# Causal convolution taps of two channel groups moved to GpSimd, their norm issued after the chunks of the sample attention, and one power operation for four row tiles

## The chip, the cores and the metric

The kernel runs on one core of a Trainium2 chip (trn2). The metric is the time of one execution in microseconds (us). A core has five engines with a queue each, which they work through in order: PE (TensorE: matmuls and transposes; PEld is its weight load), DVE (VectorE), ACT (ScalarE), POOL (GpSimd) and SP (SyncE, which here issues nearly all DMAs).

## The reference, cut to what matters

One layer of a hybrid decoder for 512 prompt rows and 64 sample rows (8 sequences of 8 new tokens). After a norm, one input projection feeds two groups. Group A is latent attention; the sample rows attend over 2048 cached keys in pages of 128. Group B is a gated linear unit, a causal depthwise convolution of width 31 over 512 channels, a norm over the channels and a swish. Both groups go through one output projection, and a gated feed-forward network follows.

```python
D_CQ = 384; D_C = 256; D_CONV = 512; CONV_W = 31
def mixer_inputs(h, pos, w_in, g_q_norm, w_uq, g_kv_norm, w_uk):
    proj = h @ w_in
    cq, ckv, kr, glu_in = ...
    q = jnp.einsum('btc,chd->bthd', rmsnorm(cq, g_q_norm), w_uq)
    kv_rows = jnp.concatenate([rmsnorm(ckv, g_kv_norm), kr], axis=-1)
    glu = glu_in[..., :D_CONV] * jax.nn.sigmoid(glu_in[..., D_CONV:])
def conv_module(glu, prev, w_dw, b_dw, g_ln, b_ln):
    y, new_prev = causal_dwconv(glu, prev, w_dw, b_dw)
    return jax.nn.silu(layernorm(y, g_ln, b_ln)), new_prev
# merge: x + concat(rmsnorm(attn), rmsnorm(conv_y)) @ w_o, then the gated network
```

`rmsnorm` and `layernorm` need the power -0.5 of a mean per row.

## The kernel before, in words

Rows come in five tiles (`TILES`: four of 128 prompt rows, one of 64 sample rows); channels of the convolution in four groups `m` of 128, one on each partition. Matmuls run on numbers split into a high and a low part, so most tiles are copied (`split`: ACT copies the high part, L110; DVE subtracts, L111).

The order of work is: input norm; the latent columns of the projection (`latent_cols`) and the GLU columns (`glu`, one group `m` at a time); the latent norms and transposes per row tile (`latent`); queries; then the sample attention; then the prompt attention by heads; the output projection; the feed-forward network, which takes the second half of the time.

The **convolution** of group `m` over the prompt is 31 taps, each a multiply-add of 512 elements on each partition (`conv_taps`, L239 to L250). On DVE a tap is one instruction (L246). On POOL it is two: the product into a temporary `ct` (L249) and the sum (L250); the first tap of a chain is one instruction (L244). The constants `NV0`, `NV2`, `NV3`, `NG2` divide the taps: group 0 has 20 on DVE and 11 on POOL into a second accumulator `acc2`; group 1 has all 31 on POOL; group 2 has 12 on DVE before the sample attention, 15 more on DVE inside it, one per chunk (the list `later`), and the last four on POOL into `acc2`; group 3 has all 31 on POOL. The chains on POOL are issued after the last power operation so far (`tc.issue_after(last["pow"])`). POOL adds `acc2` at L988 when chunk 21 comes. The sample rows' part of the convolution is `conv_sample` on DVE (L258 to L262).

The **power operation** is `rstd_of` (L116 to L120): DVE scales, POOL raises to -0.5 (L119). `latent(i)` calls it for each row tile.

The **sample attention** has 32 chunks of 512 keys (loop over `J`, `slot(J)`). A chunk transposes its keys on PE into `ktb`, splits them (`kh` on ACT, `kl` on DVE), multiplies with the queries into `sb` (L585 to L588), takes the running maximum on DVE (L592), and for the sequence before it the exponential (ACT, L607), transposes of the probabilities (`ptb`), the split of the values (`ch` on ACT, L637; `cl` on DVE, L638) and the product with the values (`ob`, L647 to L655). The pages are loaded by SP, seven chunks ahead.

The **norm of the convolution** is `conv_norm` (L746 to L781): for each row tile transposes to rows (`lnb`), statistics on DVE, a power operation on POOL, the scaling on ACT (L763), transposes back (`lnt`) and a copy on ACT (L747); then the swish (L769); then per row tile transposes (`lns`), a sum of squares (L776) and another power operation. Its steps are issued two per chunk from chunk `CN0` = 21 on. `conv_scaled` (L835, L836) makes the left operand of `proj_conv`, which projects the conv rows between the heads of the prompt attention; `wob` is its bank. The prompt attention starts with `open_right` at chunk 33, whose eight POOL memsets (L793, L794) clear parts of the value tiles `vh` and `vl` that the products `pv` read.

The tile `gx` holds the GLU output of all four groups. Its memory is given to the weights `wv` at chunk 30 (tag `gx`), which therefore wait until the taps have read it, and later to a part of the attention's output (`atp`).

The order within each engine's queue is not written out: a planner that models the engines fixes it before the run. It takes what its model says is ready, by a priority that follows the program's order, shifted by the entries of `PR` under which a step is issued (`cn` is -150, `later` +80).

Of the kernel before, what the change touches and what calls it, by code (L numbers as in the profile page):

```python
# [15 lines left out]
ALU = mybir.AluOpType  # L16
# [47 lines left out]
def hymba_step(ctx, tc, x, cache, pt, sconv, sffn, vec, rows, w1, wglu, wuq, wuk, wuv, wukT,  # L64
# [8 lines left out]
    # ------------------------------------------------------------------ helpers  # L73
# [71 lines left out]
    # ------------------------------------------------------------------ pools, first loads  # L145
# [63 lines left out]
    # ------------------------------------------------------------------ input norm  # L209
# [19 lines left out]
    gx = pcv.tile([P, 4, GE], F32, name="gx", tag="gx")  # L229
    G.memset(gx[:, :, 0:CW - 1], 0.0)  # L230
    gxs = gx[:, :, GP:].rearrange("p m (b t) -> p m b t", b=NB)
# [5 lines left out]
    def conv_taps(m, ks, E, first, dst=None):  # L237
        am = acc[:, m, 0:NP] if dst is None else dst
        for j, k in enumerate(ks):  # L239
            w = vcol("wdw", m * CW + k)  # L240
            xm = gx[:, m, k:k + NP]
# [10 lines left out]
    def conv_sample(m, E):  # L252
        w = vc[:, VEC["wdw"][0] + m * CW:VEC["wdw"][0] + (m + 1) * CW]
        for g in range(2):
            v = gxs[:, m, 4 * g:4 * g + 4, 0:CW]
# [10 lines left out]
    NV2 = 12  # L266
    NV3 = 0
    NG2 = 4
# [9 lines left out]
    def glu():  # L278
        for m in range(4):
# [11 lines left out]
            V.tensor_tensor(gx[:, m, c0:c0 + HALF], pb[0][:, :HALF], sg[:, 0:HALF], ALU.mult)  # L291
            V.tensor_tensor(gx[:, m, c0 + HALF:c0 + NP], pb[1][:, :n2], sg[:, HALF:NP], ALU.mult)
            V.tensor_tensor(gxs[:, m, :, c0:c0 + DS],
# [4 lines left out]
    # ------------------------------------------------------------------ latent columns  # L298
# [28 lines left out]
    for m in range(4):  # L327
        A.copy(gxs[:, m, :, 0:CW - 1], scs[:, m])
# [23 lines left out]

    def latent(i):
        t0, n = TILES[i]
        pi = pj[i]
        junk = tmp.tile([P, D], F32, name="junk", tag="t4")
        ss = small("ss")
        A.activation(junk[:n, :DCQ], pi[:n, :DCQ], AF.Square, scale=DCQ ** -0.5, accum_out=ss[:n, 0:1])
        A.activation(junk[:n, :DC], pi[:n, DCQ:DCQ + DC], AF.Square, scale=DC ** -0.5, accum_out=ss[:n, 1:2])
        r = rstd_of(ss[:n, 0:2], n, 2, 1.0)  # L360
# [21 lines left out]
    # ------------------------------------------------------------------ queries  # L382
# [70 lines left out]
    with prio("l4"):  # L453
        latent(4)
        split(krn[:DR, 0], krn[:DR, 1], krT[:, NP:NT])
# [3 lines left out]
    with prio("l0"):  # L459
        latent(0)  # L460
# [29 lines left out]
    def conv_state(g):  # L490
        cso = tmp.tile([P, 2, 9 * (CW - 1)], F32, name="cso", tag="t4")
        for m in range(2):
            A.copy(cso[:, m, :CW - 1], gx[:, 2 * g + m, NP:GP])
            A.copy(cso[:, m, CW - 1:].rearrange("p (b t) -> p b t", b=NB), gxs[:, 2 * g + m, :, DS:])
        nc.scalar.dma_start(oconv[:, 2 * g:2 * g + 2], cso)

    with prio("v2"):
        conv_taps(2, range(NV2), V, True)
# [7 lines left out]
    later = [(2, -1)] + [(2, k) for k in range(NV2, CW - NG2)] + [(3, -1)] + [(3, k) for k in range(CW - NV3, CW)]  # L506
    with tc.issue_after(last["pow"]):
        conv_taps(3, range(CW - NV3), G, True)
        if NG2:
            conv_taps(2, range(CW - NG2, CW), G, True, acc2)  # L510
# [3 lines left out]
    # ------------------------------------------------------------------ sample attention  # L514
# [14 lines left out]
    CN0 = 21  # L529
# [201 lines left out]
    # ------------------------------------------------------------------ convolution group: norm, silu  # L731
# [4 lines left out]
    def conv_norm():  # L736
        """steps of two halves each: at the start and at the end of a slot"""
# [45 lines left out]
    # ------------------------------------------------------------------ prompt attention  # L783
# [17 lines left out]
    def open_left():  # L801
# [5 lines left out]
        # the prompt's probabilities, later h2  # L807
# [56 lines left out]
    def proj(half, c, w, i):  # L864
        """one row tile of the output projection, in steps"""
# [38 lines left out]
    def head_in(h):  # L904
        """splits the keys and queries of head h"""
# [28 lines left out]
    def prob_T(h, j):  # L934
        """column of query q for key block k: 384 k + q, q >= 128 k"""
# [38 lines left out]
    # ------------------------------------------------------------------ order of work  # L974
    assert NV2 > 0 and len(later) <= NL * (CN0 - LS)
# [8 lines left out]
    for J in range(NJ + 6):  # L984
        if J == NJ + 1:
            open_right()
        if J == CN0 and NG2:
            G.tensor_tensor(acc[:, 2, :NP], acc[:, 2, :NP], acc2, ALU.add)  # L988
# [51 lines left out]
    R["atp"] = [pcv.tile([P, 4, NP], F32R, name="atp" + q, tag=t) for q, t in (("l", "gx"), ("h", "acc"))][::-1]  # L1040
# [52 lines left out]
    # ------------------------------------------------------------------ output projection of the attention rows  # L1093
# [45 lines left out]
    # ------------------------------------------------------------------ FFN  # L1139
# [220 lines left out]
```

## Time and profile before

Three runs took 921.27 us (median; 921.2 to 922.46). The profiled execution has a span of 919.5 us from its first to its last instruction.

| | busy us | share of the span |
|---|---|---|
| profiled execution: span | 919.5 | |
| median of the runs | 921.27 | |
| PE | 864.1 | 94% |
| DVE | 606.3 | 66% |
| ACT | 431.4 | 47% |
| POOL | 288.3 | 31% |

Busy times are sums over one engine's instructions. Matmuls are pipelined and their ends are modelled, so that a PE busy to 95% can still have room. A number in brackets such as [<-DVE kl L111] in a row of the trace is idle time of an engine before an instruction, and names what ended it.

### The profile page before, as it was taken

Reading aid. Unit: us, or ns where it says so; the run is one execution under the profiler, and the core shown is the slowest. Engines: PE = TensorE matmul, PEld = TensorE weight load, DVE = VectorE, ACT = ScalarE, POOL = GpSimd, SP = SyncE. Lnnn points to the kernel's source line nnn. Section 1 sums busy time; section 2 is a strip of 40 time slices with the busy share of each in tenths; the row PEclk is TensorE's granted clock in tenths of the full one; section 3 lists DMA queues with packets and bytes.
Section 4 is the critical chain, followed back from the end, with each engine's and each line's share of the span. In section 5 each row is a group of like instructions: output and inputs, shape, how many; then the busy total and the mean of one; then the engine's idle time right before and its main releaser. Section 6 shows DMA issues by size and latency. Waiting matters only on the chain.

```text
span 919.5 us, 15985 instructions
## 1 busy us (share of the span) xinstructions
PE 864.1 (94%) x5820; PEld 773.8 (84%) x5820; DVE 606.3 (66%) x1097; ACT 431.4 (47%) x1008; POOL 288.3 (31%) x378
## 2 busy tenths in 40 slices
PE   7997977799989999998989999999999999999995
PEld 5997867666667767876769999999999999999995
DVE  6289789899987677777675666673124667665333
ACT  6322633577758976455453334333223343333333
POOL 3076299999981110000111122110001112211222
PEclk9998989899999999999999999999999999999998
DMA  7222114454442014011233222222332223223212
GB/s 231 81 61 75 58 62 130 123 153 117 116 110 80 26 47 149 24 47 28 65 109 115 91 89 73 86 64 67 88 110 94 75 87 92 71 63 99 70 41 104
DMA packets 37651, 79.80 MB, mean 87 GB/s; under 512 B 4226, under 2 KB 21699, under 8 KB 37572
## 3 DMA queue, kind: packets, MB, share of 16 engines
q1 hardware_dynamic: 37282, 78.22, 28.2%
q8 instruction: 46, 0.75, 0.3%
q10 hardware_dynamic: 290, 0.56, 0.2%
q14 instruction: 33, 0.27, 0.1%
HBM read 74.78 MB, written 3.98 MB: 86 GB/s over the span
## 4 chain that ended last, share of the span: by engine, by line
PE 72%; POOL 18%; DVE 5%; issue 2%; ACT 2%; DMA 1%; POOLq 0%; DVEq 0%; ACTq 0%
PE ub L129 10%; PE ub L131 10%; PE ub L133 10%; POOL acc L250 10%; POOL ct L249 7%; PE db L133 5%; PE db L131 5%; PE db L129 5%; PE ob L651 2%; PE wob L123 2%; PE wob L125 2%; PE wob L124 2%; DVE acc L246 2%; PE pq L125 1%; PE pq L124 1%
## 5 line engine op out<-in xcount | busy, mean ns | idle before, releaser
L129 PE MATMUL ub<-h2h,wup_h 128*128 128x288 f32 x704 | 154.0, 296 | 0.0
L131 PE MATMUL ub<-h2l,wup_h 128*128 128x288 f32 x704 | 153.9, 295 | 0.0
L133 PE MATMUL ub<-h2h,wup_l 128*128 128x288 f32 x704 | 152.7, 294 | 0.0
L133 PEld LDWEIGHTS ub<-h2h,wup_l 128*128 128x128 f32 x704 | 114.4, 189 | 0.0
L129 PEld LDWEIGHTS ub<-h2h,wup_h 128*128 128x128 f32 x704 | 114.0, 189 | 0.2
L131 PEld LDWEIGHTS ub<-h2l,wup_h 128*128 128x128 f32 x704 | 114.2, 189 | 0.0
L111 DVE TENSOR_TENSOR wup_l<-wup_r,wup_h 128x1024 fp32r<-128x1024 f32 x44 | 53.9, 1225 | 84.0 <-ACT wup_h L110 84.0
L250 POOL TENSOR_TENSOR acc<-acc,ct 128x512 f32<-128x512 f32 x73 | 108.1, 1480 | 2.8
L1180 POOL COPY nf<-U 128x2 f32<-128x2 f32 x44 | 28.7, 652 | 216.5 <-ACT U L1178 216.5
L249 POOL TENSOR_SCALAR ct<-gx,vc 128x512 f32<-128x512 f32 x73 | 78.8, 1090 | 0.0
L119 POOL TENSOR_TENSOR rstd<-ms,mhalf 128x1 f32<-128x1 f32 (+3 forms) x25 | 17.1, 687 | 195.5 <-ACT junk L971 111.4
L131 PE MATMUL db<-gl,wdn_h 128*128 128x288 f32 x352 | 78.4, 297 | 0.0
L129 PE MATMUL db<-gh,wdn_h 128*128 128x288 f32 x352 | 78.1, 299 | 0.0
L133 PE MATMUL db<-gh,wdn_l 128*128 128x288 f32 x352 | 77.6, 297 | 0.0
L110 ACT CAST wup_h<-wup_r 128x1024 fp32r<-128x1024 f32 x44 | 46.2, 1051 | 41.3 <-PE ub L131 30.7
L111 DVE TENSOR_TENSOR wdn_l<-wdn_r,wdn_h 128x768 fp32r<-128x768 f32 (+1 forms) x32 | 28.4, 888 | 54.9 <-ACT wdn_h L110 54.9
L110 ACT CAST wdn_h<-wdn_r 128x768 fp32r<-128x768 f32 (+1 forms) x32 | 25.0, 781 | 74.7 <-PE db L131 64.2
L131 PEld LDWEIGHTS db<-gl,wdn_h 128*128 128x128 f32 x352 | 57.9, 190 | 0.0
L133 PEld LDWEIGHTS db<-gh,wdn_l 128*128 128x128 f32 x352 | 57.5, 190 | 0.0
L129 PEld LDWEIGHTS db<-gh,wdn_h 128*128 128x128 f32 x352 | 57.0, 189 | 0.0
L246 DVE SCALAR_TENSOR_TENSOR acc<-gx,vc,acc 128x512 f32<-128x512 f32 x45 | 54.2, 1204 | 0.8
L110 ACT CAST gh<-uo 128x512 fp32r<-128x512 f32 (+1 forms) x44 | 16.9, 431 | 77.8 <-DVE uo L1191 77.8
(352 smaller groups left out, 2096.6 us busy)
## 6 DMA issues: line engine op xcount, KB each, us to landing
wup_r<-in_wup_dram SPq DMA_DIRECT2D x44, 512.0 KB, 3.5
CR<-in_cache_dram SPq DMA_DIRECT2D x128, 144.0 KB, 2.2
wdn_r<-in_wdn_dram SPq DMA_DIRECT2D x16, 384.0 KB, 3.1
wdn_r<-in_wdn_dram SPq DMA_DIRECT2D x16, 320.0 KB, 2.9
x<-in_x_dram SPq DMA_DIRECT2D x8, 512.0 KB, 5.9
wg_r<-in_wglu_dram SPq DMA_DIRECT2D x8, 512.0 KB, 3.2
wo_r<-in_wo_dram SPq DMA_DIRECT2D x8, 512.0 KB, 3.5
out_y_dram<-x SPq DMA_DIRECT2D x4, 512.0 KB, 3.2
```

What stands on the lines that cost most here:

```text
L110: A.copy(hi, src)
L111: last["split"] = V.tensor_tensor(lo, src, f(hi), ALU.subtract).ins
L123: T.matmul(out, lh, rh, start=start, stop=False)
L124: T.matmul(out, lh, rl, start=False, stop=False)
L125: T.matmul(out, ll, rh, start=False, stop=stop)
L129: T.matmul(o, lh, rh, start=start, stop=False)
L131: T.matmul(o, lh, rl, start=False, stop=False)
L133: T.matmul(o, ll, rh, start=False, stop=stop)
L246: V.scalar_tensor_tensor(am, xm, w, am, ALU.mult, ALU.add)
L249: G.tensor_scalar(t, xm, w, 1.0, ALU.mult, ALU.mult)
L250: G.tensor_tensor(am, am, t, ALU.add)
L1180: G.tensor_copy(nf[:, ch, 0:2], u[:, NP:UP])
```

## The change

All 31 taps of group 2 go to POOL, ahead of the 31 of group 3; the 27 taps of group 2 on DVE, its four into `acc2` and the sum at L988 go. `gx` becomes two tiles: `gx3` for groups 0 to 2, whose memory `wv` and `atp` reuse, and `gx1` for group 3. `later` keeps only the two `conv_sample` calls, at chunks 3 and 6. `CN0` becomes 33, so that the steps of `conv_norm` are issued from chunk 33 on. The new `latent_gains` computes the sums of squares of row tiles 0 to 3 and then one power operation for all four; the sample tile 4 keeps one of its own.

```diff
+    gx3 = pcv.tile([P, 3, GE], F32, name="gx3", tag="gx3")
+    gx1 = pcv.tile([P, 1, GE], F32, name="gx1", tag="gx1")
+    gx = [gx3[:, 0], gx3[:, 1], gx3[:, 2], gx1[:, 0]]
...
+    def latent_gains(tiles):
+        n = TILES[tiles[0]][1]
+        junk = tmp.tile([P, D], F32, name="junk", tag="t4")
+        ss = small("ss")
+        for j, i in enumerate(tiles):
+            pi = pj[i]
+            A.activation(junk[:n, :DCQ], pi[:n, :DCQ], AF.Square, scale=DCQ ** -0.5, accum_out=ss[:n, 2 * j:2 * j + 1])
+            A.activation(junk[:n, DCQ:DCQ + DC], pi[:n, DCQ:DCQ + DC], AF.Square, scale=DC ** -0.5,
+                         accum_out=ss[:n, 2 * j + 1:2 * j + 2])
+        r = rstd_of(ss[:n, 0:2 * len(tiles)], n, 2 * len(tiles), 1.0)
+        for j, i in enumerate(tiles):
+            rlat[i] = r[:, 2 * j:2 * j + 2]
...
     with prio("l4"):
+        latent_gains([4])
         latent(4)
...
     with prio("l0"):
+        latent_gains([0, 1, 2, 3])
         latent(0)
...
-    with prio("v2"):
-        conv_taps(2, range(NV2), V, True)
...
-    later = [(2, -1)] + [(2, k) for k in range(NV2, CW - NG2)] + [(3, -1)] + [(3, k) for k in range(CW - NV3, CW)]
+    later = [2, 3]
     with tc.issue_after(last["pow"]):
-        conv_taps(3, range(CW - NV3), G, True)
-        if NG2:
-            conv_taps(2, range(CW - NG2, CW), G, True, acc2)
+        conv_taps(2, range(CW), G, True)
+        conv_taps(3, range(CW), G, True)
...
-    CN0 = 21
+    CN0 = 33
...
-        if J == CN0 and NG2:
-            G.tensor_tensor(acc[:, 2, :NP], acc[:, 2, :NP], acc2, ALU.add)
...
-            wv = pcv.tile([P, 2, 1024], F32R, name="wv", tag="gx")
+            wv = pcv.tile([P, 2, 1024], F32R, name="wv", tag="gx3")
...
-        for m, k in later[:NL if J >= LS else 0]:
+        for m in later[:NL if J >= LS and J % 3 == 0 else 0]:
...
-                if k < 0:
-                    conv_sample(m, V)
-                else:
-                    conv_taps(m, [k], V, False)
+                conv_sample(m, V)
```

## Rows read from the trace of the kernel before

**Rows 1.** Busy time of each engine by stretches, with the number of instructions in brackets; the columns are PE, PEld, DVE, ACT, POOL, then the granted TensorE clock, the DMA share and GB/s.

```profile
111.40:150.00 38.60, 32.44 (x206) 29.67 (x205) 34.43 (x45) 14.90 (x30) 38.05 (x30) 0.91 0.34 103
150.00:172.00 22.00, 14.50 (x84) 12.56 (x82) 18.82 (x22) 7.80 (x18) 21.69 (x18) 0.77 0.30 83
...
190.00:250.00 60.00, 57.29 (x346) 40.61 (x347) 55.50 (x108) 45.48 (x107) 59.06 (x49) 0.98 0.47 127
...
273.00:333.00 60.00, 59.36 (x367) 43.16 (x368) 42.53 (x119) 48.80 (x100) 7.01 (x12) 0.97 0.20 56
...
362.00:450.00 88.00, 84.80 (x480) 67.22 (x481) 68.29 (x164) 52.76 (x152) 0.96 (x2) 1.00 0.16 48
```

**Rows 2.** The chain of waits that ended last, from the page: share of the span by engine.

```profile
PE 72%; POOL 18%; DVE 5%; issue 2%; ACT 2%; DMA 1%; POOLq 0%; DVEq 0%; ACTq 0%
```

**Rows 3.** The last matmul of a chunk's scores (L588) over all 32 chunks: count, durations in ns (least, median, most), first and last start in us; then its busy time and count in two stretches.

```profile
L588 PE MATMUL sb<-KR,QZ x32: 388/393/628, 169.5 to 331.3; 128*128 128x512 f32 x32
...
190.00:250.00 60.00, 4.55 (x11) 0.98 0.47 127
250.00:333.00 83.00, 6.23 (x15) 0.98 0.27 74
```

**Rows 4.** DVE's groups of instructions by line, from 172 to 250 us: busy us, mean ns of one, idle time before them.

```profile
L246 DVE SCALAR_TENSOR_TENSOR acc<-gx,vc,acc 128x512 f32<-128x512 f32 x15 | 18.4, 1226 | 0.0
L638 DVE TENSOR_TENSOR cl<-CR,ch 128x512 fp32r<-128x512 f32 x12 | 12.4, 1031 | 0.0
```

**Rows 5.** The same view from 275 to 333 us.

```profile
L638 DVE TENSOR_TENSOR cl<-CR,ch 128x512 fp32r<-128x512 f32 x11 | 7.5, 678 | 2.4 <-ACT ch L637 2.4
```

**Rows 6.** The timeline from 150 to 182 us: start, length, instruction, and how many of them in a run.

```profile
149.44 11.10 DVE L246 SCALAR_TENSOR_TENSOR acc<-gx,vc,acc 128x512 f32<-128x512 f32 x8
...
162.14 1.27 DVE L111 TENSOR_TENSOR kl<-ktb,kh 128x512 fp32r<-128x512 f32 x2
...
162.87 0.80 PE L586 MATMUL sb<-kl,QL 128*128 128x512 f32 x1 [6.74 <-DVE kl L111]
```

**Rows 7.** PE's timeline where the transposes of row tile 3's latent wait, and where the convolution's norm begins.

```profile
120.86 0.40 PE L107 MATMUL ckb<-ident,pj 128*32 128x128 f32 x1 [3.83 <-DVE pj L351]
...
273.38 0.44 PE L107 MATMUL lnb<-ident,acc 128*128 128x128 f32 x2 [2.63 <-POOL acc L988]
```

**Rows 8.** Timeline rows: the write of group 1 of gx on DVE; POOL's power operations for row tiles 0 and 3 and the start of its taps; the end of its taps.

```profile
68.25 0.37 DVE L292 TENSOR_TENSOR gx<-gb,sg 128x224 f32<-128x224 f32 x1
...
92.03 0.71 POOL L119 TENSOR_TENSOR rstd<-ms,mhalf 128x2 f32<-128x2 f32 x1 [1.70 <-DVE ms L117]
...
110.72 0.69 POOL L119 TENSOR_TENSOR rstd<-ms,mhalf 128x2 f32<-128x2 f32 x1 [2.24 <-DVE ms L117]
111.41 1.14 POOL L244 TENSOR_SCALAR acc<-gx,vc 128x512 f32<-128x512 f32 x1
...
271.97 1.35 POOL L988 TENSOR_TENSOR acc<-acc,acc 128x512 f32<-128x512 f32 x1
```

**Rows 9.** The first of ACT's two squares for row tile 0 on the timeline.

```profile
89.31 0.53 ACT L358 ACTIVATE junk<-pj 128x384 f32<-128x384 f32 x1
```

**Rows 10.** Busy time of POOL in the second half of a tap (L250) in two stretches, us and count; then the same for the first half (L249).

```profile
190.00:250.00 60.00, 34.65 (x24) 0.98 0.47 127
250.00:270.00 20.00, 12.11 (x9) 1.00 0.44 119
...
190.00:250.00 60.00, 24.39 (x24) 0.98 0.47 127
250.00:270.00 20.00, 7.78 (x9) 1.00 0.44 119
```

**Rows 11.** PE's timeline through the work of one chunk.

```profile
265.28 0.40 PE L587 MATMUL sb<-KR,QZ 128*128 128x512 f32 x1
...
265.74 0.28 PE L647 MATMUL ob<-ch,PT 128*128 128x256 f32 x1
...
266.31 1.08 PE L651 MATMUL ob<-CR,PF 128*64 128x256 f32 x4
...
267.60 1.04 PE L107 MATMUL ktb<-ident,CR 128*128 128x128 f32 x8
```

**Rows 12.** Groups of the convolution's norm from 268 to 330 us: one of PE's, then ACT's.

```profile
L107 PE MATMUL lnb<-ident,acc 128*128 128x128 f32 x16 | 2.7, 283 | 2.6 <-POOL acc L988 2.6
...
L769 ACT ACTIVATE acc<-acc,vc 128x576 f32<-128x576 f32 x4 | 3.1, 859 | 0.0
L763 ACT ACTIVATE ln<-lnb,nb,rstd 128x512 f32<-128x512 f32 x4 | 3.1, 781 | 0.0
L776 ACT ACTIVATE junk<-lns 128x512 f32<-128x512 f32 x4 | 2.4, 597 | 0.9 <-PE lns L107 0.8
L747 ACT COPY acc<-lnt 128x512 f32<-128x512 f32 x4 | 2.3, 584 | 1.4 <-PE lnt L107 1.3
```

**Rows 13.** What follows the norm: the scaled conv rows; the first products of the prompt attention with the values; POOL's memsets.

```profile
L835 ACT ACTIVATE cvh<-acc,vc x4: 762/796/814, 358.5 to 365.1; 128x576 fp32r<-128x576 f32 x4
...
L123 PE MATMUL pv<-PTp,vh x32: 218/320/501, 366.5 to 446.0; 128*128 128x512 f32 x8, 128*128 128x384 f32 x8, 128*128 128x256 f32 x8, 128*128 128x128 f32 x8
...
L793 POOL MEMSET vh<- x4: 311/311/313, 326.8 to 337.1; 128x256 f32 x4
```

**Rows 14.** SP's queue from 320 to 400 us.

```profile
350.22 2.01 SPq L819 DMA_DIRECT2D x<-in_x_dram  x4
```

More of the change, by code (lines that the diff above doesn't have):

```diff
@@ L228, in hymba_step @@
     GE = GP + NB * (CW - 1 + DS)
-    gx = pcv.tile([P, 4, GE], F32, name="gx", tag="gx")
-    G.memset(gx[:, :, 0:CW - 1], 0.0)
-    gxs = gx[:, :, GP:].rearrange("p m (b t) -> p m b t", b=NB)
+    gx3 = pcv.tile([P, 3, GE], F32, name="gx3", tag="gx3")
+    gx1 = pcv.tile([P, 1, GE], F32, name="gx1", tag="gx1")
+    gx = [gx3[:, 0], gx3[:, 1], gx3[:, 2], gx1[:, 0]]
+    for t in gx:
+        G.memset(t[:, 0:CW - 1], 0.0)
+    gxs = [t[:, GP:].rearrange("p (b t) -> p b t", b=NB) for t in gx]
     scs = ps0.tile([P, 4, NB, CW - 1], F32, name="scs", tag="xt", bufs=2)
@@ L240, in conv_taps @@
             w = vcol("wdw", m * CW + k)
-            xm = gx[:, m, k:k + NP]
+            xm = gx[m][:, k:k + NP]
             if j == 0 and first:
@@ L254, in conv_sample @@
         for g in range(2):
-            v = gxs[:, m, 4 * g:4 * g + 4, 0:CW]
+            v = gxs[m][:, 4 * g:4 * g + 4, 0:CW]
             win = bass.AP(v.tensor, v.offset, [v.ap[0], v.ap[1], (1, DS), (1, CW)])
@@ L265, in hymba_step @@
     NV0 = 20
-    NV2 = 12
-    NV3 = 0
-    NG2 = 4
     NL = 1
@@ L290, in glu @@
                     yield
-            V.tensor_tensor(gx[:, m, c0:c0 + HALF], pb[0][:, :HALF], sg[:, 0:HALF], ALU.mult)
-            V.tensor_tensor(gx[:, m, c0 + HALF:c0 + NP], pb[1][:, :n2], sg[:, HALF:NP], ALU.mult)
-            V.tensor_tensor(gxs[:, m, :, c0:c0 + DS],
+            V.tensor_tensor(gx[m][:, c0:c0 + HALF], pb[0][:, :HALF], sg[:, 0:HALF], ALU.mult)
+            V.tensor_tensor(gx[m][:, c0 + HALF:c0 + NP], pb[1][:, :n2], sg[:, HALF:NP], ALU.mult)
+            V.tensor_tensor(gxs[m][:, :, c0:c0 + DS],
                             pb[1][:, n2:HALF].rearrange("p (b t) -> p b t", b=NB),
@@ L327, in hymba_step @@
     for m in range(4):
-        A.copy(gxs[:, m, :, 0:CW - 1], scs[:, m])
+        A.copy(gxs[m][:, :, 0:CW - 1], scs[:, m])
     gl = glu()
@@ L351, in rope_rows @@
         V.tensor_tensor(dst, t1[:n, :nh], t2[:n, :nh], ALU.add)
+    rlat = {}
+    def latent_gains(tiles):
[10 more added lines that the diff above has]
+            rlat[i] = r[:, 2 * j:2 * j + 2]
     def latent(i):
@@ L355, in latent @@
         pi = pj[i]
[L356 to L360, printed above, removed]
+        r = rlat[i]
         V.scalar_tensor_tensor(pi[:n, :DCQ], pi[:n, :DCQ], r[:n, 0:1], gq[:n], ALU.mult, ALU.mult)
@@ L492, in conv_state @@
         for m in range(2):
-            A.copy(cso[:, m, :CW - 1], gx[:, 2 * g + m, NP:GP])
-            A.copy(cso[:, m, CW - 1:].rearrange("p (b t) -> p b t", b=NB), gxs[:, 2 * g + m, :, DS:])
+            A.copy(cso[:, m, :CW - 1], gx[2 * g + m][:, NP:GP])
+            A.copy(cso[:, m, CW - 1:].rearrange("p (b t) -> p b t", b=NB), gxs[2 * g + m][:, :, DS:])
         nc.scalar.dma_start(oconv[:, 2 * g:2 * g + 2], cso)
-    with prio("v2"):
-        conv_taps(2, range(NV2), V, True)
     V.tensor_tensor(acc[:, 0, :NP], acc[:, 0, :NP], acc2, ALU.add)
@@ L972, in head_ss @@
                          accum_out=ssa[:, i, p_:p_ + 1])
-    assert NV2 > 0 and len(later) <= NL * (CN0 - LS)
     for J in range(NCR):
@@ L1039, in hymba_step @@
             conv_scaled(m)
-    R["atp"] = [pcv.tile([P, 4, NP], F32R, name="atp" + q, tag=t) for q, t in (("l", "gx"), ("h", "acc"))][::-1]
+    R["atp"] = [pcv.tile([P, 4, NP], F32R, name="atp" + q, tag=t) for q, t in (("l", "gx3"), ("h", "acc"))][::-1]
     def head_front(h):
```

## The prediction, made before the result was known

> **What bounds the kernel now.** I read the stretches first [rows 1], then the chain of waits, then DVE's groups. From 190 to 250 us, inside the sample attention, DVE is busy 55.5 of 60 us, ACT 45.5 and POOL 59.1; PE shows 57.3, but a busy PE still has room. In that stretch 11 chunks pass, 5.5 us each, and from 250 to 333 us 15 more, again 5.5 us each [rows 3]. In the first half DVE is what a chunk waits for. Of its work from 172 to 250 us, 18.4 us are 15 taps [rows 4]. In the second half the taps are gone but the norm of the convolution has come in, and ACT is busy 48.8 of 60 us. The chain of waits gives POOL 18% of the span [rows 2]: its taps run without a break from 111.4 to 273.3 us [rows 8], and PE waits 2.6 us for them when the norm begins [rows 7]. So two things run side by side there: chunks paced by DVE and then ACT, and a chain on POOL. From 362 us on PE is busy 84.8 of 88 us and paces the rest.
>
> **The change part by part.** The sum is made against the profiled execution: a span of 919.5 us, with 1.8 us around it up to the median of 921.27.
>
> A. *Group 2's first 12 taps leave DVE.* Eight of them stand in a row from 149.4 to 160.5 us, while the first chunk's keys wait for DVE's split; PE waits 6.7 us for `kl` [rows 6]. Afterwards TensorE is at its lower clock (1.2 of 2.4 GHz) for a while: 0.77 granted on the mean of 150 to 172 us, against 1.00 later [rows 1]. The 6.7 us go. For the clock I add 2.3 us: five of the 22 us were lost to it ((1 - 0.77) x 22), about half of that while PE had work. That makes **-9**. Ends: 0, if the writes of `gx`'s last group, which stand behind the taps, are late for another reason; -11.1, the length of the eight taps. I stay near the row of the wait itself.
>
> B. *The 15 taps inside the chunks leave DVE, and the norm leaves the chunks.* Without 12 taps of 1.23 us DVE has 40.8 us to do in the stretch from 190 to 250 us, ACT 45.5: ACT's 45.5/11 = 4.1 us a chunk is then the longest of the two. In the second half ACT loses the norm's squares, copies, scalings and swish, 2.4 + 2.3 + 3.1 + 3.1 us [rows 12]. PE needs about 4.1 us for keys (1.04), six score matmuls at 0.23 and the values (0.57 + 1.08) [rows 11], and by my estimate 0.3 more for the probabilities' transposes and the rest: 4.4 us. Three engines at 4.1 to 4.4 us don't reach the 92% that DVE reached when it alone was behind. I take 4.8 us a chunk (4.4 at 92%). For the 26 chunks of 5.5 us that is **-18**. Ends: 4.4 us, PE alone, -29; 5.2 us, half of the first half's gain and none later, -8. One cost against it stands in the rows: DVE's `cl` takes 1031 ns beside POOL's taps and 678 ns after them [rows 4, 5], and POOL now runs beside all chunks. For the last 11 that is 11 x 0.35 = 3.9 us of DVE, which has room for it and which 4.8 us takes in.
>
> The Trainium skill, "SBUF — State Buffer", section "Who interferes with whom", puts this harder: a DVE instruction with two SBUF inputs and a GpSimd instruction that reads SBUF shut each other out for their whole length. If each of these 11 waited for a whole second half of a tap (1.44 us), 16 us of DVE would come instead of 3.9; with half of these 12 us hidden in DVE's room, the sum below would be -12 instead of -18. The trace agrees that there is such a wait, but with 0.35 us.
>
> C. *One power operation for four tiles.* Row tiles 0 and 3 get theirs at 92.0 and 110.7 us [rows 8]. ACT's squares for four tiles, two each and by my estimate 1.4 us a tile from the 0.53 us of the first, start at 89.3 us [rows 9]; so the one operation comes at about 97 us. Tile 0 is 5 us later, under queued GLU matmuls; tiles 2 and 3 are earlier, and the 3.8 us for which PE waits for tile 3 at 120.9 us [rows 7] should shrink: **-2**. Ends: -4, the whole wait; +2, DVE's small steps now standing beside POOL's taps from 98 us on. Three operations of 0.7 us on POOL go, in its idle time.
>
> D. *The norm behind the chunks.* It goes from stretches where DVE or ACT was behind to one where PE is. Its three passes of 20 transposes cost, at 2.7 us for 16 [rows 12], about 10 us of PE, some of it the modelled ends: **+8**. Ends: +6, +15 (ACT's 11 us and the steps' round trips show too).
>
> E. *POOL's chain is longer.* POOL loses four taps and the sum, gains 31: 93 taps in three chains instead of 66. A pair took (34.65 + 24.39)/24 = 2.46 us beside DVE's taps and (12.11 + 7.78)/9 = 2.21 us after them [rows 10]; I take 2.3. Group 1 of `gx` is written at 68 us [rows 8], so the chain may start after the power operation, at 98 us, not 111. It ends at 98 + 2.7 + 90 x 2.3 = 308 us (299 to 322). The chunks end at 331.3 - 9 - 18 - 2 = 302 us. What waits behind POOL's taps: the norm with its own power operations, and the eight memsets [rows 13] without which the products `pv`, at 366.5 us before, can't start. The temporary `ct` also lies on memory given to later tiles; if the rows `x` take it, SP's loads of them [rows 14] wait too, and what SP has queued behind. Meanwhile PE has values, keys and scores of the first heads. The scaled conv rows began at 358.5 us [rows 13]; the norm has thus some 50 us after 308. I take **+3** for fewer filling matmuls between the first heads. Ends: 0, +15.
>
> The split of `gx` I cost at nothing: `wv` waits for groups 0 to 2 alone, done one chain (some 71 us) before POOL ends; without the split it would wait until 308 us, past its use. The `conv_sample` call that moves from late chunks to chunk 6 does the same work.
>
> Sum: -9 - 18 - 2 + 8 + 3 = **-18**: span 901.5, time **903 us**.
>
> **The rivals.**
> 1. *PE stands in front of POOL (slower).* Queues are in order, and the planner fixed PE's. In the old order the norm's first transposes stood within chunk 21 and PE met POOL's end within 2.6 us [rows 7], which speaks for a good model. But a chain of 93 taps gives 40% more room for its error. If the transposes stand at chunk 33 with nothing ahead, PE waits from 302 us to POOL's end. If the chain still starts at 111 us and pairs stay at 2.46 us, that is 336 us: 34 us. A, B, C and D are -21, so it decides from 21 us on (POOL done after 323 us). Price: -21 + 34 = +13, so 934 us.
> 2. *The chunks hardly speed up.* The second half had no taps on DVE and still took 5.5 us a chunk; against it, the norm was there. With 5.2 us: -9 - 8 - 2 + 8 + 3 = -8, so 913 us.
> 3. *PE alone paces the chunks, POOL speeds up.* 4.4 us a chunk, POOL at 2.2 us a pair and done first: -11 - 29 - 4 + 6 = -38, so 883 us. Against it: three engines nearly level.
> 4. *The change doesn't do what it says:* the planner keeps the norm among the last chunks and lets POOL pace them; gains and losses cancel, 921 us.
>
> **How the numbers follow.** Forecast 0.49 (own range 894 to 910), rival 1 0.14, rival 2 0.20, rival 3 0.12, rival 4 0.05. The range of 8 in 10 goes from rival 3 to short of the worst of rival 1: 884 to 924. A measurement of this kernel tells 0.2% (1.8 us) from no change. Faster: 0.49 + 0.20 + 0.12 = 0.81; same 0.05; slower 0.14.
>
> **What would show it.** A: no wait of several us for the first `kl`. B: chunks at 4.8 us, DVE below 85% in them. C: one power operation of eight columns near 97 us, POOL's taps from 98 us. D: transposes of the norm after the last chunk. E: POOL's last tap near 308 us and no wait of PE above 5 us for it; a wait above 20 us there, or chunks still at 5.4 us, would make the prediction wrong.

## The result, and the profile after

The kernel with the change took **935.29 us** (median of 4 runs, 933.08 to 935.69) against 921.4 before on the same chip: 1.4% slower, ratio 1.014 with a 95% interval of 1.0123 to 1.0156. The forecast was 903 us. The profiled execution has a span of 933.2 us, 13.7 more than before.

Four groups of instructions cut the span into parts that answer to the prediction's steps. First the kernel after: the transposes of the chunks' keys (`ktb`), the chunks' maxima (`S`), the first products `pv` of the prompt attention, the first matmuls `ub` of the feed-forward network (count, ns, first and last start in us).

```profile
L107 PE MATMUL ktb<-ident,CR x256: 270/273/477, 160.5 to 316.8; 128*128 128x128 f32 x128
...
L603 DVE CUSTOM_DVE_ANT_0 S<-sb,sl x32: 671/675/684, 168.8 to 326.3; 64x512 f32<-64x512 f32 x32
...
L123 PE MATMUL pv<-PTp,vh x32: 221/321/797, 378.8 to 460.7; 128*128 128x512 f32 x8, 128*128 128x384 f32 x8, 128*128 128x256 f32 x8, 128*128 128x128 f32 x8
...
L129 PE MATMUL ub<-h2h,wup_h x704: 290/295/607, 495.0 to 846.1; 128*128 128x288 f32 x176
```

The same groups of the kernel before, as far as they don't stand in [rows 13]:

```profile
L107 PE MATMUL ktb<-ident,CR x256: 270/273/421, 154.0 to 323.1; 128*128 128x128 f32 x128
...
L592 DVE CUSTOM_DVE_ANT_0 S<-sb,sl x32: 664/673/684, 172.6 to 332.4; 64x512 f32<-64x512 f32 x32
...
L129 PE MATMUL ub<-h2h,wup_h x704: 290/295/607, 480.4 to 832.3; 128*128 128x288 f32 x176
```

| part of the span | before | after | difference | step, forecast |
|---|---|---|---|---|
| to the first keys | 154.0 | 160.5 | +6.5 | C, -2 |
| first keys to first maximum | 18.6 | 8.3 | -10.3 | A, -9 |
| first to last chunk's maximum | 159.8 | 157.5 | -2.3 | B, -18 |
| last maximum to first `pv` | 34.1 | 52.5 | +18.4 | D, +8 |
| first `pv` to first `ub` | 113.9 | 116.2 | +2.3 | E, +3 |
| the rest | 439.1 | 438.2 | -0.9 | |

They add up to the 13.7. A and E came as forecast in this table, and three steps failed. Two of the stretches of [rows 1] and one more, of the kernel after (PE, PEld, DVE, ACT, POOL, clock, DMA share, GB/s), and between them the last score matmul of the chunks (L599) from 190 to 250 us:

```profile
150.00:172.00 22.00, 20.95 (x143) 18.21 (x141) 10.25 (x20) 9.86 (x23) 21.61 (x21) 1.00 0.35 97
190.00:250.00 60.00, 56.29 (x341) 40.59 (x340) 49.30 (x96) 43.92 (x105) 59.06 (x55) 0.97 0.48 134
...
190.00:250.00 60.00, 4.37 (x11) 0.97 0.48 134
...
350.00:370.00 20.00, 14.96 (x107) 10.76 (x105) 6.98 (x30) 15.73 (x31) 3.84 (x7) 0.74 0.40 145
```

From 150 to 172 us the granted clock is 1.00 now, against 0.77, and PE 95% busy: step A. From 190 to 250 us DVE fell from 55.5 to 49.3 us, yet the chunks still come 11 in 60 us. From 350 to 370 us PE lost 5 us to idleness, at a clock of 0.74, with ACT the busiest engine. POOL did what was forecast. Its timeline, and its groups from 111.4 to 306.4 us:

```profile
95.45 1.66 POOL L119 TENSOR_TENSOR rstd<-ms,mhalf 128x8 f32<-128x8 f32 x1 [5.89 <-DVE ms L117]
97.10 1.15 POOL L247 TENSOR_SCALAR acc<-gx,vc 128x512 f32<-128x512 f32 x1
...
303.65 2.64 POOL L253 TENSOR_TENSOR acc<-acc,ct 128x512 f32<-128x512 f32 x2
...
L253 POOL TENSOR_TENSOR acc<-acc,ct 128x512 f32<-128x512 f32 x86 | 121.1, 1408 | 3.3
L252 POOL TENSOR_SCALAR ct<-gx,vc 128x512 f32<-128x512 f32 x84 | 70.5, 850 | 0.0
```

One power operation, taps from 97 us, the last one done at 306.3 us (forecast 98 and 308), 1.41 + 0.85 = 2.26 us a pair (forecast 2.3). In the chain of waits POOL fell from 18% [rows 2] to 1%:

```profile
PE 78%; DVE 13%; ACT 4%; issue 3%; DMA 1%; SPq 1%; POOL 1%; POOLq 0%; DVEq 0%; ACTq 0%
```

So the 18% before stood for a chain that ran beside a PE with about as much to do (57.3 of 60 us [rows 1]): with POOL off the chain, PE (72% to 78%) and DVE (5% to 13%) stand in its place. Now ACT's timeline where the time went:

```profile
356.58 1.28 ACT L780 ACT_TABLE_LOAD   x1
357.88 3.14 ACT L780 ACTIVATE acc<-acc,vc 128x576 f32<-128x576 f32 x4
361.58 0.60 ACT L787 ACTIVATE junk<-lns 128x512 f32<-128x512 f32 x1 [0.56 <-PE lns L107]
...
366.13 1.28 ACT L936 ACT_TABLE_LOAD   x1
367.43 0.37 ACT L936 ACTIVATE Pm<-spb,nm 128x128 f32<-128x128 f32 x1
...
368.91 0.78 ACT L846 ACTIVATE cvh<-acc,vc 128x576 fp32r<-128x576 f32 x1
```

The norm's transposes began at 330.9 us, behind the last chunk. Its swish, with a table load ahead and another behind, its sums of squares and only then the first exponential `Pm` of the prompt attention stand here in a row, at 367.4 us.

### The profile page after: what moved, and what is told of

Same layout as the page of the kernel before. It is cut to its first block, busy times and chain, and to the rows that moved or that the text cites. A ratio compares the mean times of both kernels' runs of the same rounds, so it can differ in the third digit from the quotient of the medians.

```text
span 933.2 us, 16013 instructions
## 1 busy us (share of the span) xinstructions
PE 875.4 (94%) x5820; PEld 781.5 (84%) x5820; DVE 591.5 (63%) x1067; ACT 433.4 (46%) x1008; POOL 334.4 (36%) x431
## 4 chain that ended last, share of the span: by engine, by line
PE 78%; DVE 13%; ACT 4%; issue 3%; DMA 1%; SPq 1%; POOL 1%; POOLq 0%; DVEq 0%; ACTq 0%
PE ub L129 10%; PE ub L131 10%; PE ub L133 10%; PE db L131 5%; PE db L129 5%; PE db L133 5%; PE ob L662 3%; PE ktb L107 2%; PE wob L123 2%; PE wob L125 2%; PE wob L124 2%; DVE acc L249 2%; PE gb L129 2%; PE gb L131 1%; PE gb L133 1%
## 5 line engine op out<-in xcount | busy, mean ns | idle before, releaser
L133 PE MATMUL ub<-h2h,wup_l 128*128 128x288 f32 x704 | 152.5, 294 | 0.0
L253 POOL TENSOR_TENSOR acc<-acc,ct 128x512 f32<-128x512 f32 x100 | 143.4, 1434 | 3.8
L252 POOL TENSOR_SCALAR ct<-gx,vc 128x512 f32<-128x512 f32 x100 | 90.8, 919 | 0.0
L111 DVE TENSOR_TENSOR kl<-ktb,kh 128x512 fp32r<-128x512 f32 x64 | 42.6, 682 | 14.1 <-ACT kh L110 13.5
```

Of the source, the lines that this page charges most:

```text
L111: last["split"] = V.tensor_tensor(lo, src, f(hi), ALU.subtract).ins
L133: T.matmul(o, ll, rh, start=False, stop=stop)
L252: G.tensor_scalar(t, xm, w, 1.0, ALU.mult, ALU.mult)
L253: G.tensor_tensor(am, am, t, ALU.add)
```

## The experiments

All were timed in three rounds beside the kernel before, whose median was 921.0 to 922.1 us in each set. Ratios are to it, with 95% intervals.

**The norm's place, moved to chunk 27** (the kernel after):

```diff
-    CN0 = 33
+    CN0 = 27
```

> The changed kernel with the norm issued from chunk 27 instead of 33; nothing else differs. In the changed kernel POOL's last tap ends at 306 us, when chunk 27 passes, but the norm's first transposes stand at 331 us and its last step at 366 us, with PE busy only 15 of 20 us from 350 to 370. Theory 1 (the norm's chain of short steps stands exposed behind the chunks): most of the 12 us that the first product pv comes later than before is won back, 923 us (919 to 927), PE waits no more than 5 us for POOL at the norm's start. Rival (POOL's long chain, not the place of the norm, is the cost): PE now meets POOL's end, waits, and the time stays at 932 us or more.

937.98 us, 1.0179 (1.0156 to 1.0203): slower still. The norm now stood among the last chunks, with POOL's end at 305 us (PE waited 2.1 us for it), and its two table loads (at 334 and 341 us) fell among their last exponentials; the first `pv` came at 379.4 us. "Right behind POOL's end" is not what the norm wants.

**One power operation per tile** (the kernel after):

```diff
-        latent_gains([0, 1, 2, 3])
+        latent_gains([0])
...
-                latent(i + 1)
+                latent_gains([i + 1])
+            latent(i + 1)
```

> The changed kernel with one power operation per row tile again; POOL's taps of group 1 then start behind the last of them, near 111 us. Theory 2 (POOL's taps from 97 us on slow DVE's small two-input steps of the latents and the queries, and PE loses 6 us before the sample attention): the GLU matmuls of group 2 start near 130 us instead of 136, and the time falls by 3 to 6 us, to 929 to 932 us, although POOL ends 13 us later (near 320 us, still before the norm at 331 us). Rival (the early start costs nothing, the loss is all behind the chunks): 935 us or, with POOL later, more.

929.6 us, 1.0086 (1.0064 to 1.0108): 5.7 us better than the kernel after, and the first keys are back at 154.5 us. (The edit also takes the other tiles' latents out of the priority `l1`, which the kernel before gives them.) Part C has the wrong sign. POOL ends at 318 us instead of 306 and PE still doesn't wait for it.

**Both together:**

> The changed kernel with the norm issued from chunk 27 and one power operation per row tile. POOL then ends near 320 us, 13 us after chunk 27. Theory: the two gains do not add, since POOL's end is now what the norm waits for: PE stands 5 to 13 us or the norm slips into the last chunks; 918 to 930 us. Rival (the two parts are independent): the sum of the gains of the two single runs.

949.43 us, 1.0307 (1.0289 to 1.0325): far above both expectations. Here rival 1's mechanism is real. PE's timeline:

```profile
315.97 0.48 PE L107 MATMUL lnb<-ident,acc 128*128 128x128 f32 x1 [20.05 <-POOL acc L253]
```

PE stood 20 us in front of POOL. In the kernel after no such wait is in PE's list.

**What in C costs: the shared operation, or POOL's early start?** The kernel after with its shared operation, and POOL held until 106.2 us by one small operation ahead of its taps, which reads what DVE writes there:

```diff
+        last["pow"] = G.tensor_tensor(small("hold")[:NS, 0:1], qr4[:NS, 0, 0, 0:1], mhalf[:NS], ALU.mult).ins
         b = bank("qrb", "x")
```

> The kernel after with its shared power operation, but with one small POOL operation ahead of the taps that reads the sample queries' repeated rope part, which DVE writes at about 111 us: POOL's taps start there as in the kernel before, instead of at 97 us. Theory (POOL's taps, which slow DVE's small operations between 97 and 111 us, cost the front its 6 us): the first keys are transposed at about 155 us instead of 160.5, but POOL ends at about 319 us, so 929 to 932 us as with one power operation per tile. Rival (the shared operation itself costs them: all four tiles' scalings come at once at 97 us, 7 us later than the first one before, ahead of the split of the query weights): the first keys stay at 159 us or later, and with POOL's end at 319 us the time is 936 us or more.

929.09 us, 1.0075 (1.0047 to 1.0102); the first keys at 155.6 us. The theory holds: 4.9 of the 6.5 us go with POOL's early start (kernels with one and the same front have their first keys up to 2.1 us apart, 152.4 to 154.5 us, so the 4.9 is good to about that). DVE's timeline, first of the kernel after:

```profile
97.14 0.63 DVE L373 SCALAR_TENSOR_TENSOR pj<-pj,rstd,gq 128x384 f32<-128x384 f32 x1 [1.77 <-POOL rstd L119]
...
100.24 1.65 DVE L373 SCALAR_TENSOR_TENSOR pj<-pj,rstd,gq 128x384 f32<-128x384 f32 x1
101.82 1.49 DVE L379 SCALAR_TENSOR_TENSOR pj<-pj,rstd,gkv 128x256 f32<-128x256 f32 x1
103.23 1.35 DVE L111 TENSOR_TENSOR wuq_l<-wuq_r,wuq_h 128x1152 fp32r<-128x1152 f32 x1
```

and with POOL held:

```profile
98.74 0.61 DVE L373 SCALAR_TENSOR_TENSOR pj<-pj,rstd,gq 128x384 f32<-128x384 f32 x1
99.27 0.48 DVE L379 SCALAR_TENSOR_TENSOR pj<-pj,rstd,gkv 128x256 f32<-128x256 f32 x1
99.66 1.35 DVE L111 TENSOR_TENSOR wuq_l<-wuq_r,wuq_h 128x1152 fp32r<-128x1152 f32 x1
```

Beside POOL's taps the scalings of `pj` take up to 1.65 us instead of 0.61, and the split of the query weights behind them comes 3.6 us later (0.5 of it because the scalings began later); PE waits for that split 2.5 us, and with POOL held 0.3. That is the rule of the Trainium skill that the prediction weighed for the chunks ("SBUF — State Buffer", "Who interferes with whom"). The rows agree that there is such a wait, up to 1.04 us here, only it decided elsewhere: in the front, where DVE's small steps were on the path.

**What paces the chunks?** First the kernel before with the 15 taps on DVE inside its chunks left out:

```diff
-                else:
-                    conv_taps(m, [k], V, False)
```

> The kernel before with the 15 taps of group 2 that DVE does inside the chunks left out (so the convolution of group 2 lacks 15 of its 31 taps); nothing is put in their place. Theory 3 (PE, not DVE, paces the chunks, and the taps stand beside its work): at most 4 us are won, 917 to 921 us, and chunks still pass every 5.2 to 5.5 us from 190 to 250 us with DVE well below 90% busy. Rival (step B of the prediction: DVE paces them): 15 x 1.23 us less on DVE give 8 us or more, 913 us or less.

914.36 us, 0.9922 (0.99 to 0.9945): 6.9 us, 0.46 us a tap instead of 1.23. That is more than the theory's 4 us and less than the rival's 8. By the 21st of the 32 chunks' maxima 4.3 us were won (264.4 instead of 268.7 us); behind it POOL ended at 263.4 us instead of 273.3 and let the norm begin sooner, and what that is worth by itself was not taken apart. Then one score matmul less per chunk, in the kernel before:

```diff
-        T.matmul(s, qz[:, i], KR[:, 0], start=False, stop=False)
-        T.matmul(s, qz[:, i], KR[:, 1], start=False, stop=True)
+        T.matmul(s, qz[:, i], KR[:, 0], start=False, stop=True)
```

> The kernel before with one of the eight score matmuls of each chunk left out (the low part of the rope keys, the last matmul of the scores; the scores lose that term): 32 matmuls, which at 0.23 us of pitch are 7.4 us less for PE and nothing less for DVE, ACT or POOL. Theory (PE paces the chunks in both kernels, which is why 15 taps less on DVE gave so little): 914 to 916 us, the chunks from 250 to 330 us at about 5.3 instead of 5.5 us. Rival (DVE or the round trips between engines pace them): 919 us or more.

927.83 us, 1.0067 (1.0046 to 1.0088): slower than before with less work. The number lies in the rival's range, but neither theory had that. PE came to the norm's transposes at 265.9 instead of 270.3 us and waited 5.7 us there for POOL; the first `pv` came 4.6 us later than before. As a time it says little of the pace, but its chunks do: the first maximum came 4.8 us sooner than before and the 20th 4.8 us sooner too, so that 19 matmuls less on PE won nothing between them, though the clock took some there (0.83 instead of 0.97 granted from 170 to 190 us). So the first half of the kernel before is not shown to be paced by PE, and DVE's 18.4 us of taps are worth at most the 4.3 us above. Next POOL emptied, in the kernel after:

```diff
-        conv_taps(2, range(CW), G, True)
-        conv_taps(3, range(CW), G, True)
+        conv_taps(2, range(1), G, True)
+        conv_taps(3, range(1), G, True)
```

> The kernel after with all but the first tap of groups 2 and 3 left out, so that POOL has nothing to do from about 170 us on and DVE has no taps either; the norm stays behind the chunks. Theory (POOL's taps slow DVE's operations with two SBUF operands, but in the second half of the chunks PE paces): the chunks from 190 to 250 us go at 5.0 us instead of 5.45, those from 250 to 328 us stay near 5.0 to 5.1, the last chunk's maximum comes at 318 to 324 us, and the time is 924 to 931 us. Rival (POOL's stream beside DVE is what keeps the chunks at 5.2 to 5.5 us): 4.7 us in both halves, the last maximum before 315 us, 922 us or less. Second rival (PE paces all chunks): no more than 2 us gained, 933 us or more.

934.59 us, 1.013 (1.0092 to 1.0167; single runs 928.6 to 937.0): no gain clear of this spread, the second rival's case. From 190 to 328 us:

```profile
190.00:250.00 60.00, 56.18 (x343) 40.86 (x342) 42.67 (x100) 44.27 (x104) 0.00 (x0) 0.96 0.47 132
250.00:328.00 78.00, 74.93 (x447) 54.23 (x447) 51.46 (x127) 52.02 (x113) 0.31 (x1) 0.96 0.29 83
```

DVE is busy 43 of 60 us, ACT 44, POOL not at all, and first to last maximum take 156.5 us instead of 157.5. Of the engines only PE is still nearly full, and the last run takes the same score matmul out of the kernel after:

> The kernel after with one of the eight score matmuls of each chunk left out (the low part of the rope keys; the scores lose that term): 32 x 0.23 = 7.4 us less for PE. The same edit in the kernel before gave nothing at the middle of the chunks, where DVE's taps are also behind. Theory (in the kernel after, with no taps on DVE, PE paces the chunks): the last chunk's maximum at 321 to 323 us instead of 328.4, 927 to 930 us. Rival (the round trips between PE, ACT and DVE pace them): the last maximum at 326 us or later, 932 us or more.

928.16 us, 1.0073 (1.0046 to 1.0101), 7.1 us less than the kernel after. The chunks' maxima:

```profile
L602 DVE CUSTOM_DVE_ANT_0 S<-sb,sl x32: 669/673/685, 167.6 to 319.1; 64x512 f32<-64x512 f32 x32
```

The last comes 7.2 us sooner, about what was taken out (31 x 0.23 us). But that is in part a coincidence. 1.2 us are there at the first maximum already. And from 250 to 328 us the kernel after (first row) had a lower granted clock than this run (second row):

```profile
250.00:328.00 78.00, 75.11 (x443) 53.78 (x442) 60.89 (x129) 52.41 (x113) 55.58 (x53) 0.96 0.29 83
...
250.00:328.00 78.00, 74.63 (x459) 52.59 (x458) 61.48 (x142) 58.25 (x125) 58.80 (x61) 1.00 0.29 83
```

The lower clock stands at 275 to 280 us (0.69) and 280 to 285 us (0.63), after PE had been busy 4.0 of the 5 us before; that is 3.4 us. The run with a matmul less had PE busy 4.0 of the same 5 us and no such fall; what makes the difference no run shows. The kernel after without its norm (below) has the same chunks and 1.00 from 250 us on, and takes 154.1 us from first to last maximum; with a matmul less it is 151.5, in the kernel after 157.5. So at the same clock the matmul is worth some 2.6 us of 7.1, which fits a second half paced by PE: PE is busy 75.1 of 78 us there, and its rows through a chunk show no idle time (point B below). Only 1.4 us were won by the 20th of the 32 maxima. In the first half the chain of waits of the kernel after goes through three engines in turn (its shares by line, from 190 to 250 us):

```profile
by line: PE ob L662 13.0%; DVE cl L649 10.8%; DVE kl L111 8.5%; PE ktb L107 7.5%; issue 4.8%; PE sb L596 4.8%; DVE ol L676 4.7%; PE sb L597 4.2%; PE ptb L107 3.6%; DVE cs L261 3.6%; DVE S L603 3.0%; ACT S L618 3.0%; ACT ch L648 2.9%; PE ob
```

By the 20th maximum neither POOL emptied nor a matmul less gave more than 1.4 us; what a chunk waits for in the first half (by this chain it would be round trips between the engines) no run has shown.

**The norm, left out in both kernels** (its scales set to one):

```diff
-    cn = conv_norm()
+    cn = iter(())
+    V.memset(rc, 1.0)
```

> The kernel after without the norm of the convolution: its transposes, statistics, scaling, swish and sums of squares are left out, and the conv rows' scales are set to one. Theory (behind the chunks the norm has nothing to hide it: from the last chunk to the first products of the prompt attention there are 50.4 us instead of 32.1): 915 to 919 us, some 18 us less than the kernel after. Rival (the norm's work costs the same wherever it stands, and the loss is elsewhere): at most 12 us less, 923 us or more.

> The kernel before without the norm of the convolution, as in the run beside this one. Theory (among the chunks part of the norm is hidden): 909 to 914 us, 8 to 12 us less than the kernel before, so that the norm's place accounts for 6 to 10 us of the loss. Rival (its cost is the same in both kernels): 18 us less, 903 us.

After: 913.52 us, 0.9928 (0.991 to 0.9945). Before: 913.0 us, 0.9926 (0.99 to 0.9952). **Without the norm both kernels take the same time.** Leaving it out wins 21.8 us where it stands behind the chunks and 8.0 us where it stands among them, and the difference of 13.8 is as much as the loss; what the change wins and loses elsewhere cancels. Of the 21.8 us, 4.0 are won by the last chunk's maximum, ahead of the norm's first step, 3.4 of them by the clock as above. The chunks' maxima and the first `pv`, after and then before:

```profile
L603 DVE CUSTOM_DVE_ANT_0 S<-sb,sl x32: 669/674/684, 168.2 to 322.3; 64x512 f32<-64x512 f32 x32
...
L123 PE MATMUL pv<-PTp,vh x32: 221/322/792, 357.7 to 439.1; 128*128 128x512 f32 x8, 128*128 128x384 f32 x8, 128*128 128x256 f32 x8, 128*128 128x128 f32 x8
```

```profile
L592 DVE CUSTOM_DVE_ANT_0 S<-sb,sl x32: 669/673/684, 171.0 to 319.9; 64x512 f32<-64x512 f32 x32
...
L123 PE MATMUL pv<-PTp,vh x32: 223/320/797, 356.5 to 436.7; 128*128 128x512 f32 x8, 128*128 128x384 f32 x8, 128*128 128x256 f32 x8, 128*128 128x128 f32 x8
```

From the last maximum to `pv` it is 35.4 us, where the kernel after took 52.5, and 36.6 where the one before took 34.1: D's loss is the norm. The kernel before without its norm, with its 15 taps on DVE, goes through its chunks in 148.9 us, 4.8 each, against 154.1 in the kernel after, without taps and without the norm. From the first keys (152.5 and 159.3 us) to the last maximum it is 167.4 against 163.0: A and the taps of B together are worth 4.4 us.

**The norm early again.** The kernel after with 15 of group 2's taps left out, so that POOL ends where it did before, and `CN0 = 21`:

> The kernel after with the last 15 of group 2's taps on POOL left out (so its sums are short of them) and the norm issued from chunk 21 on, as before the change. POOL's chains then end at about 272 us, as in the kernel before. Theory (what the change loses in the middle is the room in which the norm can hide, not POOL's or DVE's work itself): the norm runs from about 272 to 325 us among the chunks, the first products of the prompt attention come at about 366 us, and the time is 917 to 922 us: the 935 of the kernel after, less 12 to 15. Rival (the loss is a general slowdown by POOL's longer stream and the front, and the place of the norm matters little): 930 us or more.

926.9 us, 1.0056 (1.0039 to 1.0072): 8.4 us better, short of the 12 to 15 expected. First `pv` at 371.2 us instead of 366.5. The first keys still come 6.2 us later than in the kernel before, but the first maximum comes 4.0 us sooner; then the chunks, with the norm among them again, take 167.1 us instead of 159.8, with a wait of PE for POOL of 4.7 us instead of 2.6.

**Written later.** With one power operation per tile (929.6 us): the steps 300 places later in the planner's order; written behind the first scores and the sample attention's own values; spread over the first head. The last two also have `cn=0` and `CN0 = 99`, and the last one projects the conv rows from the second head on.

```diff
-cn=-150
+cn=150
```

> The kernel after with one power operation per tile (929.6 us) and the norm's steps 300 places later in the planner's order, behind the first heads of the prompt attention instead of ahead of them. Theory (the first heads lose 12 us because their maxima and exponentials stand in DVE's and ACT's queues behind the norm's steps): the first products of the prompt attention come at 366 to 368 us instead of 377, the norm's work fills gaps between the heads, and the time is 918 to 924 us. Rival (the norm's work needs its 15 to 20 us wherever it stands, or the projection of the conv rows is then too late to fill between the heads): 928 us or more.

```diff
-    CN0 = 33
+    CN0 = 99
...
     with prio("aT"):
         sample_T()
+    with prio("cn"):
+        for _ in cn:
+            pass
     with prio("cv"):
```

> The kernel after with one power operation per tile (929.6 us), and all steps of the norm written behind the first scores and exponentials of the prompt attention and behind the sample attention's own values, rows and transposes, instead of ahead of them. Theory (behind the chunks, what costs is that the norm's steps stand in PE's, ACT's and DVE's queues ahead of work that doesn't need them): the first prompt exponentials come within 15 us of the last chunk's maximum instead of 36, and 918 to 925 us. Rival (the norm's chain is needed by the conv rows' products, which stand ahead of the first products of the attention, so its length counts wherever it stands): 928 to 932 us.

```diff
+            if h == 0:
+                with prio("cn"):
+                    next(cn, None)
+                    next(cn, None)
```

> As the run beside this one, but the norm's steps are spread over the first head of the prompt attention, two per part of the head, and the conv rows' products come from the second head on. Theory (the norm hides if PE, ACT and DVE have other work between its steps): 912 to 920 us, below the kernel before, with the first products of the attention at 355 to 360 us. Rival (TensorE's work and the two loads of ACT's tables count wherever they stand, since PE paces the heads as well): 922 to 930 us.

934.79 us (1.0134, 1.0105 to 1.0164), 930.23 (1.0079, 1.0062 to 1.0096) and 937.51 (1.0152, 1.013 to 1.0173). My theory that the queues' order was the cost fell. The second of them did bring the exponentials forward; ACT's timeline, and what PE then did (the third had its first `pv` at 354.4 us, about as expected, and the longest time of the three):

```profile
338.78 0.37 ACT L937 ACTIVATE Pm<-spb,nm 128x128 f32<-128x128 f32 x1
```

```profile
345.00:370.00 25.00, 15.41 (x62) 10.18 (x61) 9.95 (x27) 16.81 (x26) 3.86 (x7) 0.59 0.14 43
```

The first exponential comes 22 us sooner than with the norm ahead of it (361.2 us in the kernel of 929.6 us), and the first `pv` at 379.6 us instead of 377.0 all the same: while the norm went from engine to engine, PE was busy 15.4 of 25 us at a clock of 0.59. My reading, not tested, is that the early work was done by then and nothing dense was left beside the norm.

**Versions that might beat both.** The kernel before with eight of its first 12 taps behind the first keys' split:

```diff
-        conv_taps(2, range(NV2), V, True)
+        conv_taps(2, range(4), V, True)
...
+    with prio("v2"), tc.issue_after(last["kl"][0]):
+        conv_taps(2, range(4, NV2), V, False)
```

> The kernel before with eight of group 2's first 12 taps on DVE issued behind the split of the first chunk's keys instead of ahead of it; all else as before. Theory (the only gain of the change that came through is the wait for the first keys, 6.7 us of which 3.8 to 6 arrived at the first chunk; eight more taps among the chunks cost 0.46 us each): the first maximum at 167 to 169 us instead of 172.6, 918 to 921 us. Rival (DVE is behind in the first chunks, and the taps cost there what they cost before): 922 us or more, with the 21st chunk as late as before.

921.35 us, 0.9999 (0.9983 to 1.0015): PE's wait for `kl` only moved, 7.8 us at a later split. And the opposite of the change (`NG2 = 0`, `NL = 2`, `CN0 = 19`):

> The opposite of the change, in the kernel before: group 2's last four taps go from POOL to DVE too (19 taps among the chunks, two per chunk from the third on), so that POOL's chain is some 12 us shorter, and the norm is issued from chunk 19 on. Theory (the earlier the norm, the more of its 8 us is hidden; DVE has 4.9 us more to do in the first half): POOL ends at 258 to 264 us, 917 to 920 us. Rival (DVE then paces the first half and POOL is slowed by its taps, so nothing is won): 922 us or more.

925.31 us, 1.0042 (1.0027 to 1.0056): POOL ended at 266.5 us, 6.8 us sooner instead of 12 (its pairs took 2.63 us from 190 to 250 us, beside more of DVE's taps, instead of 2.46 [rows 10]), and the last maximum came 2.4 us later. No version that does all the work beats the kernel before.

## Why the prediction was wrong, point by point

- **A (forecast -9)**: -10.3 us at the first maximum, with the wait gone and the clock at 1.00. But it did not last. Against the kernel before the first maximum came 3.8 us sooner and the fifth 0.9 us sooner (187.5 instead of 188.5 us). Ahead of it PE stood for the transposes of the next sequence's rope keys (`krb`), which by the chain of waits stood behind a copy on ACT and a page of the cache that landed at 178.8 us; the granted clock was 0.50 from 180 to 185 us, after PE had been busy 2.5 of the 5 us before. From PE's list of waits:

```profile
PE krb L107 <- ACT RP L561: 2.5, 1, 2.5
```

  Without the norm, A and the taps of B are 4.4 us at the last maximum.
- **B (-18) failed.** "In the first half DVE is what a chunk waits for" was wrong (18.4 us of taps were worth at most 4.3 there), and so was PE at 4.4 us a chunk; its own sign of being wrong, chunks still at 5.4 us, came with 11 in 60 us. I read the bound from busy shares, dismissed PE's 57.3 of 60 us since "a busy PE still has room", and put all of its smaller matmuls at 0.3 us. (The end of -8 was 26 x 0.3 us; "half of the first half's gain" would have been 4.) One chunk on PE's timeline of the kernel after, from the first score matmul to that of the next chunk:

```profile
305.80 0.50 PE L596 MATMUL sb<-kh,QL 128*128 128x512 f32 x1
...
307.31 0.27 PE L107 MATMUL krb<-ident,RP 128*128 128x128 f32 x1
307.42 1.04 PE L107 MATMUL ktb<-ident,CR 128*128 128x128 f32 x8
308.29 0.49 PE L107 MATMUL krb<-ident,RP 128*128 128x128 f32 x3
308.54 0.36 PE L658 MATMUL ob<-ch,PT 128*128 128x256 f32 x1
...
309.21 0.65 PE L662 MATMUL ob<-CR,PF 128*64 128x256 f32 x2
309.79 0.24 PE L124 MATMUL snb<-ckvl,QL 128*64 128x64 f32 x1
309.96 0.65 PE L662 MATMUL ob<-CR,PF 128*64 128x256 f32 x2
310.54 0.24 PE L125 MATMUL snb<-ckvh,QL 128*64 128x64 f32 x1
...
311.16 0.48 PE L596 MATMUL sb<-kh,QL 128*128 128x512 f32 x1
```

  No row has an idle time before it: 5.36 us (5.2 on the mean of the 15 chunks from 250 to 328 us), 1.3 more than the 4.1 I had for scores, keys and values. What comes once per four chunks (the rope keys `krb` and the new tokens' scores `snb` in this one, their probabilities `pnb` and the output `olb` in others) or two (`ptb`) is more than a remainder. Of B only the norm's leaving was real: without it the kernel before goes 159.8 - 148.9 = 10.9 us faster through its chunks. Of that the change kept 2.3: its chunks without the norm take 5.2 us more (154.1; they start 2.8 us sooner and end 2.4 later), and 3.4 more with the norm behind them, as much as the lower clock at 275 to 285 us.
- **C (-2) failed in sign**: +6.5. Its bound of +2 named the cause, DVE's small steps beside POOL's taps, and sized it too low; 4.9 us of it go when POOL is held.
- **D (+8) failed in size**: +18.4. I counted PE's transposes. Without the norm the stretch is 35.4 us instead of 52.5, so 17.1 of it are the norm's. What counts behind the chunks is the chain: transposes, statistics on DVE, power on POOL, scaling on ACT, transposes, copy, swish with two table loads, squares, with PE idle and at a lower clock meanwhile. My end of +15 ("ACT's 11 us and the steps' round trips show too") named the cause and was still too low. Its counterpart, what the norm cost among the chunks, I had inside B at no figure of its own: it is 8.0 us.
- **E (+3)**: +2.3, with POOL's end and pair as worked out. That it comes from fewer filling matmuls is not shown.
- **Rival 1** gave 934 us with a chance of 0.14, and 935 came, but not by its mechanism, so the agreement is chance: POOL was done 24.6 us before PE's first transposes of the norm (330.9 us). Rival 2 (5.2 us a chunk) was right on the pace (157.5 us for 31 steps are 5.1).

The split of the norm's 21.8 us among PE's idle time, its lower clock and its 60 transposes was not taken apart.

## What to carry to other kernels

Work with many hand-overs between engines costs much less while another stage keeps the bounding engine full (here 8.0 us instead of some 18); before such work is moved, ask what will run beside it there, and price its whole chain, not one engine's share. Where several engines are nearly full in a stage (here 76 to 95%), add up every matmul of one period on the timeline, the ones that come every second or fourth period too, before calling the fullest other engine the bound. Giving an idle engine work sooner is not free if instructions on the path take longer beside that work.

## What the runs showed of the hardware

POOL and DVE slow each other here, and the runs give both sizes. DVE's split of the values, from 190 to 250 us in the kernel after, and with POOL emptied:

```profile
L649 DVE TENSOR_TENSOR cl<-CR,ch 128x512 fp32r<-128x512 f32 x12 | 12.8, 1071 | 3.6 <-ACT ch L648 3.6
```

```profile
L649 DVE TENSOR_TENSOR cl<-CR,ch 128x512 fp32r<-128x512 f32 x12 | 8.2, 681 | 3.9 <-ACT ch L648 3.9
```

390 ns each, which cost the chunks nothing that the run could tell. The other way, a pair on POOL took 2.46 us beside DVE's 15 taps [rows 10] and 2.14 us with them left out, from 190 to 250 us:

```profile
L250 POOL TENSOR_TENSOR acc<-acc,ct 128x512 f32<-128x512 f32 x28 | 37.6, 1342 | 1.1
L249 POOL TENSOR_SCALAR ct<-gx,vc 128x512 f32<-128x512 f32 x29 | 22.9, 799 | 0.0
```

That is 0.32 us a pair by which taps on DVE make a chain on POOL later.
